# First norm and first products of a diffusion block: latent tokens ahead of context tokens, parameters loaded ahead of x

## The chip, the cores and the metric

The kernel runs on one core of a Trainium2 chip. Its engines are TensorE (PE, the matrix products; its weight loads are listed as PEld), VectorE (DVE), ScalarE (ACT), GpSimd (POOL) and SyncE (SP, which here only issues DMA transfers). The metric is the device time of one execution in microseconds; a profiled execution adds a trace in which every instruction has a start and a duration.

## The reference, cut to what matters

Two token streams share all weights: 512 latent tokens x (modulated by c) and 256 context tokens ctx (modulated by c_ctx). The change lies in the first sub-layer of layer 0, ahead of the convolutions:

```python
sh1, sc1, g1, sh2, sc2, g2 = adaln(c[:, None, :], w_mod[l], b_mod[l])   # silu(c) @ w_mod + b_mod
csh1, csc1, cg1, csh2, csc2, cg2 = adaln(c_ctx, w_mod[l], b_mod[l])
h = modulate(rmsnorm(x, norm_mix[l]), sh1, sc1)        # x * rsqrt(mean(x*x)) * gain * (1 + scale) + shift
hc = modulate(rmsnorm(xc, norm_mix[l]), csh1, csc1)
y = conv_mixers(h, w_in_ab[e], ...)                    # p = h @ w_in; v_b * sigmoid(gate_b); ...
yc = conv_mixers(hc, w_in_ab[e], ...)
```

The norm, the modulation and the products with `w_in` work on each token by itself, so latent and context tokens may be taken together or one after the other.

## The kernel before, in words

The activations lie transposed: x is eight tiles `x[k]` of 128 channels by 776 columns. Columns 0 to 511 are the latent tokens (`LAT`), 520 to 775 the context tokens (`CTXS`), and 8 columns of zeros lie between (`C0` = 520, `T` = 776).

`setup` issues all DMA transfers from SP's queue: the eight x tiles (L121), the parameters `par` (L122), the identity (L124). Behind them follow, in the order of the program, the first piece of modulation weights `wm0` (four transfers of 512 KB, L222), three tiles of `w_in` (L165), and three more pieces of `wm0`.

`start` then does the first norm and the first products. ACT squares each x[k] and DVE adds the squares up in `ss` (`square_in`, L279 to L284). `rstd` multiplies `ss` by ones on PE in chunks of 128 tokens (L291), ACT takes the means out of PSUM (L294), DVE finds the inverse root by a start value and three Newton rounds (`inverse`, L296 to L301), lays it on a diagonal `rd` (L313), and PE spreads it over all 128 partitions (L323); ACT copies the result to `r` (L432). `piece(q)` makes shift and scale of channel tiles 2q and 2q+1: 32 small products with the silu of c and c_ctx (L226), a copy (L231), a transpose (L232), a copy (L234), and on DVE `mod` (L235) and `gain` (L266).

`weights` splits each fp32 weight tile in `whi` (ACT cast, L159) and `wlo` (DVE subtract, L160), and `mod_in` does the same for the modulated activations: `xr` = x*r (L336), times gain plus shift (L345, L346, or L348), then a high part and a low part (L159, L160, or L350). Each product is three matmuls, wlo*h, whi*hl, whi*h (L177 to L179). The first three slots of PSUM take the first three column tiles of `w_in` together, tile k by tile k. Then `glu` needs the first two slots: ACT takes the sigmoid of slot two (`sg`, L561), DVE multiplies it with slot one (`ub`, L570), and this frees slot one, for which the next product waits.

Each engine works through its instructions in a fixed order, which a scheduler of the language sets at build time from the program's order and its own estimate of durations. An instruction that waits holds up all behind it on its engine.

Of the kernel before, what the change touches and what calls it, by code (L numbers as in the profile page):

```python
# [12 lines left out]
F32 = mybir.dt.float32  # L13
# [7 lines left out]
P = 128  # L21
DM = 1024
KT = DM // P
SEQ = 512
CTX = 256
GRID_W = 64
C0 = SEQ + 8
T = C0 + CTX
TW = 896
# [9 lines left out]
LAT = (0, SEQ)  # L39
CTXS = (C0, T)  # L40
# [18 lines left out]
class Kern:  # L59
# [52 lines left out]
    def setup(self):  # L112
        nc, a = self.nc, self.a
        self.cst = self.pool("cst")
        self.wts = self.pool("wts")
        self.tmp = self.pool("tmp", 2)

        self.par = self.cst.tile([P, NPAR + 64], F32, name="par")[:, :NPAR]
        self.x = [self.cst.tile([P, T], F32, name=f"x{k}") for k in range(KT)]
        for k in range(KT):  # L120
            nc.sync.dma_start(self.x[k], a["x"][:, k, :])  # L121
        nc.sync.dma_start(self.par, a["par"])  # L122
        self.ident = self.cst.tile([P, P], F32, name="ident")
        nc.sync.dma_start(self.ident, a["ident"])  # L124
        self.onesm = self.cst.tile([P, P], F32, name="onesm")
        nc.vector.memset(self.onesm, 1.0)
        self.ones2 = self.cst.tile([P, 2], F32, name="ones2")
        nc.vector.memset(self.ones2, 1.0 / DM)
        self.ones2b = self.cst.tile([P, 2], F32, name="ones2b")
        nc.vector.memset(self.ones2b, 2.0 / DM)  # L130

        self.mod = self.cst.tile([P, 2, 48, 2], F32, name="mod")

        self.gain = self.cst.tile([P, 4, KT, 2], F32, name="gain")
        self.csil = self.cst.tile([P, KT, 2], F32, name="csil")
        nc.scalar.activation(self.csil, self.p("cc").rearrange("p (k c) -> p k c", c=2), AF.Silu)
# [275 lines left out]
    def start(self, ph):  # L412

        nc, a = self.nc, self.a
        segs = [LAT, CTXS]
        self.new_ss()
        for k in range(KT):
            self.square_in(k, 0, T)
        sl = [self.slot() for _ in range(3)]
        ms = self.slot()  # L420
        nc.vector.memset(ms[:, 0:P], 0.0)

        def piece(q):
            room = lambda _: ph.tile([P, 2, 512], F32, name="wmod", tag="wmod", bufs=14)
            for _ in self.mod_piece(0, 0, 16, 2 * q, a["wm0"][q], ms[:, 0:P], ms[:, 768:768 + P], room):
                pass
            self.make_gain(0, 0, 1, self.p("nmix")[:, 0:8], 2 * q, 2 * q + 2)

        piece(0)
        rp = self.rstd(self.ss, segs, self.ones2, sl[0], eng=nc.vector, pool=ph)  # L430
        r = self.tmp.tile([P, T], F32, name="r", tag="ss", bufs=1)
        nc.scalar.copy(r, rp)  # L432
        room = [[ph.tile([P, DM], F32R, name=t) for t in ("whi0", "wlo0")], None, None]
        first = [self.weights(a["w_in"][m], into=room[m]) for m in range(3)]
        piece(1)
        h = self.new_h()
        for q in range(4):
            for k in (2 * q, 2 * q + 1):
                self.mod_in(h, k, r, 0, 0, 0, segs)
            for k in (2 * q, 2 * q + 1):  # L440
                for s, w in zip(sl, first):
                    self.wide_gemm(s, w, h, segs, [k])
            if q == 0:
                piece(2)
                piece(3)
        return h, sl
# [76 lines left out]
    def spread(self, seg, project=None):  # L523

        r = self.tmp.tile([P, SEQ], F32, name="r", tag="r", bufs=1)[:, :seg[1] - seg[0]]
        s, others = self.taken()
        self.turn(others)
        self.nc.scalar.copy(r, self.rstd(self.ss, [seg], self.ones2, s, project=project))
        i = self.slot_i % len(others)
        self.turn(others[i:] + others[:i] + [s])  # L530
        return r
# [530 lines left out]
```

## Time and profile before

| what | value |
|---|---|
| time, median of 3 runs | 1472.5 us (1471.82 to 1473.2) |
| the profiled execution, its own time | 1473.53 us |
| its span, first to last instruction | 1471.8 us |
| PE busy | 1435.4 us, 98% of the span |
| DVE busy | 1024.4 us, 70% |
| ACT busy | 596.9 us, 41% |
| DMA, mean | 110 GB/s, 33.4% of 16 engines |

The span is the time between the first and the last instruction; the execution's own time is 1.73 us longer. PE is busy nearly throughout, so time is lost mostly where PE is not yet running or waits. The trace is read at the start of the program, up to about 60 us.

### The profile page before, as it was taken

Reading aid. Unit: us, or ns where it says so; the run is one execution under the profiler, and the core shown is the slowest. Engines: PE = TensorE matmul, PEld = TensorE weight load, DVE = VectorE, ACT = ScalarE, POOL = GpSimd, SP = SyncE. Lnnn points to the kernel's source line nnn. Section 1 sums busy time; section 2 is a strip of 40 time slices with the busy share of each in tenths; the row PEclk is TensorE's granted clock in tenths of the full one; section 3 lists DMA queues with packets and bytes.
Section 4 is the critical chain, followed back from the end, with each engine's and each line's share of the span. In section 5 each row is a group of like instructions: output and inputs, shape, how many; then the busy total and the mean of one; then the engine's idle time right before and its main releaser. Section 6 shows DMA issues by size and latency. Waiting matters only on the chain.

```text
span 1471.8 us, 21937 instructions
## 1 busy us (share of the span) xinstructions
PE 1435.4 (98%) x8786; PEld 1228.8 (83%) x8786; DVE 1024.4 (70%) x1635; ACT 596.9 (41%) x983; POOL 47.8 (3%) x186
## 2 busy tenths in 40 slices
PE   5999999999999999999999999999999999999997
PEld 3888888888888888888888878768799888888887
DVE  6699998689977756456434689786676865655456
ACT  5421224463223223133123475786764442424245
POOL 0000001110000000000000110010001000000000
PEclk9999999999999999999999999999999999999999
DMA  9325433134544532333211324011155333233222
GB/s 374 111 70 173 158 115 130 31 113 146 168 132 127 186 106 81 120 125 91 81 47 43 106 91 125 14 40 58 42 174 163 90 112 98 84 114 97 94 80 74
DMA packets 52709, 161.25 MB, mean 110 GB/s; under 512 B 6400, under 2 KB 6528, under 8 KB 52480
## 3 DMA queue, kind: packets, MB, share of 16 engines
q1 hardware_dynamic: 52608, 159.87, 33.4%
q8 instruction: 68, 1.11, 0.3%
q14 instruction: 33, 0.27, 0.1%
HBM read 155.13 MB, written 2.10 MB: 107 GB/s over the span
## 4 chain that ended last, share of the span: by engine, by line
PE 91%; DVE 4%; ACT 2%; issue 1%; DMA 1%; POOL 1%; DVEq 0%; SPq 0%; ACTq 0%; POOLq 0%
PE slot L177 21%; PE slot L178 21%; PE slot L179 21%; PE av L178 3%; PE av L177 3%; PE av L179 3%; PE av L929 2%; PE pt L919 2%; PE s L900 2%; PE pt L179 2%; PE pt L178 2%; PE pt L177 2%; PE slot L226 1%; PE slot L212 1%; PE slot L208 1%
## 5 line engine op out<-in xcount | busy, mean ns | idle before, releaser
L177 PE MATMUL slot<-h,wlo 128*128 128x512 f32 (+1 forms) x1192 | 410.5, 346 | 2.2 <-DVE ub L570 1.2
L178 PE MATMUL slot<-h,whi 128*128 128x512 f32 (+1 forms) x1192 | 410.8, 345 | 0.2 <-DVE h L350 0.2
L179 PE MATMUL slot<-h,whi 128*128 128x512 f32 (+1 forms) x1192 | 410.8, 345 | 0.0
L159 ACT CAST whi<-wraw 128x1024 fp32r<-128x1024 f32 (+2 forms) x215 | 192.2, 902 | 208.5 <-PE slot L179 109.3
L177 PEld LDWEIGHTS slot<-h,wlo 128*128 128x128 f32 x1192 | 223.5, 188 | 34.3 <-issue 2.0
L178 PEld LDWEIGHTS slot<-h,whi 128*128 128x128 f32 x1192 | 224.1, 188 | 29.0 <-DVE h L350 0.5
L179 PEld LDWEIGHTS slot<-h,whi 128*128 128x128 f32 x1192 | 224.1, 188 | 27.6
L160 DVE TENSOR_TENSOR wlo<-wraw,whi 128x1024 fp32r<-128x1024 f32 (+2 forms) x215 | 222.2, 1040 | 25.1 <-ACT whi L159 24.6
L370 DVE SCALAR_TENSOR_TENSOR cf<-slot,par,cf 128x775 f32<-128x775 f32 (+1 forms) x132 | 122.7, 932 | 136.5 <-ACT cf L368 136.0
L177 PE MATMUL slot<-gh,wlo 128*128 128x512 f32 (+1 forms) x459 | 156.7, 342 | 0.7 <-DVE x L360 0.4
L178 PE MATMUL slot<-gl,whi 128*128 128x512 f32 (+1 forms) x459 | 155.5, 339 | 0.0
L179 PE MATMUL slot<-gh,whi 128*128 128x512 f32 (+1 forms) x459 | 155.1, 339 | 0.0
L368 ACT ACTIVATE cf<-slot,par 128x776 f32<-128x776 f32 (+1 forms) x66 | 55.3, 837 | 243.1 <-PE slot L179 230.7
L360 DVE SCALAR_TENSOR_TENSOR x<-slot,mod,x 128x256 f32<-128x256 f32 (+1 forms) x139 | 81.8, 618 | 73.6 <-PE slot L179 73.4
L578 DVE SCALAR_TENSOR_TENSOR cacc<-ub,par,cacc 128x783 f32<-128x783 f32 x120 | 118.6, 1040 | 0.2
L254 DVE CUSTOM_DVE_ANT_0 junk<-wmod,cb 128x1024 bf16<-128x1024 f32 x80 | 97.7, 1221 | 10.2 <-DMA wmod<-in_wmt 6.6
L177 PEld LDWEIGHTS slot<-gh,wlo 128*128 128x128 f32 x459 | 86.1, 188 | 12.0 <-DVE wlo L160 0.7
L178 PEld LDWEIGHTS slot<-gl,whi 128*128 128x128 f32 x459 | 86.4, 188 | 10.3 <-DVE mod L235 0.2
L179 PEld LDWEIGHTS slot<-gh,whi 128*128 128x128 f32 x459 | 86.4, 188 | 10.1
L907 DVE CUSTOM_DVE_ANT_0 sm<-s,mask,nsink 128x640 f32<-128x640 f32 (+1 forms) x58 | 46.8, 820 | 15.9 <-PE pt L919 12.4
L704 ACT ACTIVATE sgf<-cf 128x776 f32<-128x776 f32 (+1 forms) x44 | 32.7, 744 | 60.9 <-DVE cf L370 60.4
L910 ACT ACTIVATE sm<-sm,nm 128x513 f32<-128x513 f32 (+1 forms) x64 | 50.1, 786 | 10.6 <-DVE nm L907 5.6
(244 smaller groups left out, 2246.4 us busy)
## 6 DMA issues: line engine op xcount, KB each, us to landing
wraw<-in_w_up SPq DMA_DIRECT2D x88, 512.0 KB, 3.6
wmod<-in_wmt SPq DMA_DIRECT2D x56, 512.0 KB, 4.2
wmod<-in_wm SPq DMA_DIRECT2D x40, 512.0 KB, 5.3
wraw<-in_w_down SPq DMA_DIRECT2D x48, 256.0 KB, 2.6
wraw<-in_w_in SPq DMA_DIRECT2D x20, 512.0 KB, 4.0
wraw<-in_w_down SPq DMA_DIRECT2D x32, 320.0 KB, 2.9
wraw<-in_w_o SPq DMA_DIRECT2D x16, 512.0 KB, 3.4
wraw<-in_w_out SPq DMA_DIRECT2D x16, 256.0 KB, 3.4
```

Source lines behind the costliest of these rows:

```text
L159: self.act_mark = self.nc.scalar.copy(hi, src)
L160: self.mark = self.nc.vector.tensor_tensor(lo, src, hi.bitcast(F32), op=ALU.subtract)
L177: mm(out, lo, xh, start=first, stop=False)
L178: mm(out, hi, xl, start=False, stop=False)
L179: self.product = mm(out, hi, xh, start=False, stop=last)
L254: nc.vector.tensor_tensor_reduce(junk, w, self.cb[:, c, :], 1.0, 0.0, ALU.mult, ALU.add, col)
L360: self.nc.vector.scalar_tensor_tensor(self.x[k][:, lo:hi], acc, self.mod[:, l, chunk * 8 + k, c:c + 1], self.x[k][:, lo:hi], op0=ALU.mult, ...
L368: nc.scalar.activation(acc[:, :n], u[:, :n], AF.Copy, scale=w[:, 1:2])
L370: nc.vector.scalar_tensor_tensor(acc[:, o], u[:, i], w[:, j:j + 1], acc[:, o], op0=ALU.mult, op1=ALU.add)
L578: self.tapped = nc.vector.scalar_tensor_tensor(acc, ub[:, t:t + CB_N], w[:, t:t + 1], acc, op0=ALU.mult, op1=ALU.add)
L907: scored = nc.vector.tensor_tensor_reduce(sm[:, :n], s[:, SEQ - nl:SEQ + CTX], mk, -SCALE, nsink[:, hd:hd + 1], ALU.add, ALU.min, nm)
L910: self.scored = scored, nc.scalar.activation(sm[:, :n + 1], sm[:, :n + 1], AF.Exp, scale=-1.0, bias=nm, accum_out=z)
```

## The change: what it does

`par` is issued first. Each x tile comes in two transfers, latent columns of all eight tiles first and then columns 512 to 775 of all eight. The squares, the inverse root and the spread are done for the latent tokens; the squares of the context tokens are issued after the latent means, and their inverse root and spread come inside the loop, behind the latent products of k = 0 and 1. From then on each pair of channel tiles is modulated and multiplied for the latent tokens and then for the context tokens. Lines of the changed kernel stand 1 to 10 below those of before.

```diff
         self.x = [self.cst.tile([P, T], F32, name=f"x{k}") for k in range(KT)]
-        for k in range(KT):
-            nc.sync.dma_start(self.x[k], a["x"][:, k, :])
         nc.sync.dma_start(self.par, a["par"])
+        for lo, hi in (LAT, (SEQ, T)):
+            for k in range(KT):
+                nc.sync.dma_start(self.x[k][:, lo:hi], a["x"][:, k, lo:hi])
...
         for k in range(KT):
-            self.square_in(k, 0, T)
+            self.square_in(k, *LAT)
...
         piece(0)
-        rp = self.rstd(self.ss, segs, self.ones2, sl[0], eng=nc.vector, pool=ph)
-        r = self.tmp.tile([P, T], F32, name="r", tag="ss", bufs=1)
-        nc.scalar.copy(r, rp)
+        r = ph.tile([P, TW], F32, name="r")
+
+        def spread(seg, slot):
+            nc.scalar.copy(r[:, slice(*seg)], self.rstd(self.ss, [seg], self.ones2, slot, eng=nc.vector, pool=ph))
+
+        spread(LAT, sl[0])
+        with self.tc.issue_after(self.means.ins):
+            for k in range(KT):
+                self.square_in(k, *CTXS)
...
         for q in range(4):
-            for k in (2 * q, 2 * q + 1):
-                self.mod_in(h, k, r, 0, 0, 0, segs)
-            for k in (2 * q, 2 * q + 1):
-                for s, w in zip(sl, first):
-                    self.wide_gemm(s, w, h, segs, [k])
+            for seg in segs:
+                if q == 0 and seg == CTXS:
+                    spread(seg, sl[0][:, C0:])
+                for k in (2 * q, 2 * q + 1):
+                    self.mod_in(h, k, r[:, slice(*seg)], 0, 0, 0, [seg])
+                for k in (2 * q, 2 * q + 1):
+                    for s, w in zip(sl, first):
+                        self.wide_gemm(s, w, h, [seg], [k])
             if q == 0:
                 piece(2)
                 piece(3)
```

On DVE, between the last latent square and the inverse root, stood one run of adds and one run of Newton steps before (`ss` is the sum of squares, `ry` and `rt` the Newton variables):

```order
-L284 TENSOR_TENSOR ss<-ss,sq 128x776 x7
-L296 TENSOR_SCALAR ry<-rv 128x6
-L298 TENSOR_TENSOR rt<-ry 128x6
-L299 TENSOR_TENSOR rt<-rt,rv 128x6
-L300 TENSOR_SCALAR rt<-rt 128x6
-L301 TENSOR_TENSOR ry<-rt,ry 128x6
```

Now, at the same place on DVE:

```order
+L285 TENSOR_TENSOR ss<-ss,sq 128x512 x7
+L297 TENSOR_SCALAR ry<-rv 128x4
+L299 TENSOR_TENSOR rt<-ry 128x4
+L300 TENSOR_TENSOR rt<-rt,rv 128x4
+L285 TENSOR_TENSOR ss<-ss,sq 128x256
+L301 TENSOR_SCALAR rt<-rt 128x4
+L285 TENSOR_TENSOR ss<-ss,sq 128x256
+L302 TENSOR_TENSOR ry<-rt,ry 128x4
+L285 TENSOR_TENSOR ss<-ss,sq 128x256
```

The seven adds of the context squares (two of them shown last) stand between the Newton steps of the latent tokens.

On PE, behind the products of k = 1 (the rows named `h,whi`), the third modulation piece (L226 x32) and the products of k = 2 followed before:

```order
-L177 MATMUL slot_102<-h,wlo 128x256
-L178 MATMUL slot_102<-h,whi 128x256
-L179 MATMUL slot_102<-h,whi 128x256
-L226 MATMUL slot_103<-wmod,csil 2x128 x32
-L177 MATMUL slot_100<-h,wlo_212 128x512
-L177 MATMUL slot_101<-h,wlo 128x512
```

Now, behind the latent products of k = 1 on PE (slot_108 to slot_110 are the three slots, slot_111 the modulation's):

```order
+L179 MATMUL slot_110<-h,whi 128x512
+L180 MATMUL slot_110<-h,whi 128x512
+L292 MATMUL slot_108<-ones_94,ss 128x2 x2
+L233 MATMUL slot_111<-ident,modsb 128x128
+L227 MATMUL slot_111<-wmod,csil 2x128 x32
+L233 MATMUL slot_111<-ident,modsb 128x128
+L324 MATMUL slot_108<-rd,onesm 128x256
+L227 MATMUL slot_111<-wmod,csil 2x128 x32
+L178 MATMUL slot_108<-h,wlo_239 128x256
```

The context sums (L292) and the context spread (L324) now stand in PE's queue with two modulation pieces around them, ahead of the context products of k = 0 and with no other product between.

On ACT, behind the context spread, the queue now reads:

```order
+L434 COPY r<-slot_108 128x256
+L346 ACTIVATE h<-xr,mod,gain 128x256 x2
+L160 CAST whi<-wraw 128x1024
+L232 COPY modsb<-slot_111 128x128
+L349 ACTIVATE ht<-xr,mod,gain 128x512 x2
+L160 CAST h<-ht 128x512
```

The latent modulation of k = 2 and 3 (L349) and its first high part (L160, `h<-ht`) stand behind the context tokens' copy, the context high parts and the cast of the fourth weight tile.

## Rows read from the trace of the kernel before

**Rows 1.** The page's slices: busy tenths of PE in 40 equal parts.

```profile
PE   5999999999999999999999999999999999999997
```

**Rows 2.** Timeline, 0 to 30 us: start, duration, engine, line, count, idle before.

```profile
9.18 5.25 DVE L284 TENSOR_TENSOR ss<-ss,sq 128x776 f32<-128x776 f32 x5 [0.94 <-ACT sq L283]
...
14.49 2.72 PE L291 MATMUL slot<-ones,ss 128*128 128x2 f32 x12 [14.49 <-DVE ss L284]
...
17.14 3.47 PE L226 MATMUL slot<-wmod,csil 128*2 128x128 f32 x64
...
17.45 0.17 DVE L296 TENSOR_SCALAR ry<-rv 128x6 int32<-128x6 int32 x1 [3.02 <-ACT rv L294]
...
20.08 0.96 DVE L313 TENSOR_TENSOR rd<-ident,ry 128x768 f32<-128x768 f32 x1
...
20.96 3.49 DVE L160 TENSOR_TENSOR wlo<-wraw,whi 128x1024 fp32r<-128x1024 f32 x3
...
21.18 1.53 PE L323 MATMUL slot<-rd,onesm 128*128 128x512 f32 x4 [0.58 <-DVE rd L313]
...
22.08 1.05 ACT L159 CAST whi<-wraw 128x1024 fp32r<-128x1024 f32 x1 [0.19 <-DMA wraw<-in_w_in]
...
23.04 0.80 ACT L432 COPY r<-slot 128x776 f32<-128x776 f32 x1
...
26.51 1.66 DVE L346 TENSOR_SCALAR ht<-xr,gain,mod 128x512 f32<-128x512 f32 x4
...
28.08 0.96 DVE L350 TENSOR_TENSOR h<-ht,h 128x776 fp32r<-128x776 f32 x1
...
29.10 0.50 PE L178 MATMUL slot<-h,whi 128*128 128x512 f32 x1 [0.21 <-DVE h L350]
```

**Rows 3.** Groups by shape, 0 to 60 us: busy us, mean ns, idle before.

```profile
L570 DVE TENSOR_TENSOR ub<-slot,sg 128x512 f32<-128x512 f32 x1 | 0.7, 692 | 5.9 <-ACT sg L561 5.9
...
L570 DVE TENSOR_TENSOR ub<-slot,sg 128x256 f32<-128x256 f32 x1 | 0.4, 415 | 0.0
...
L348 ACT ACTIVATE ht<-xr,mod,gain 128x512 f32<-128x512 f32 x6 | 4.9, 811 | 1.6 <-DVE gain L266 1.6
L159 ACT CAST h<-ht 128x776 fp32r<-128x776 f32 x6 | 4.7, 836 | 0.0
L348 ACT ACTIVATE ht<-xr,mod,gain 128x264 f32<-128x264 f32 x6 | 3.6, 597 | 0.0
```

**Rows 4.** Timeline, 57 to 60 us: the end of the first products.

```profile
57.65 0.82 ACT L561 ACTIVATE sg<-slot 128x776 f32<-128x776 f32 x1 [5.06 <-PE slot L179]
57.68 0.39 PE L179 MATMUL slot<-h,whi 128*128 128x512 f32 x1
...
57.91 0.28 PE L177 MATMUL slot<-h,wlo 128*128 128x256 f32 x1
...
58.03 0.28 PE L178 MATMUL slot<-h,whi 128*128 128x256 f32 x1
...
58.15 0.28 PE L179 MATMUL slot<-h,whi 128*128 128x256 f32 x1
...
59.58 0.50 PE L177 MATMUL slot<-h,wlo 128*128 128x512 f32 x1 [1.15 <-DVE ub L570]
```

**Rows 5.** Timeline, 30 to 80 us: a whole modulation piece on PE.

```profile
35.02 1.93 PE L226 MATMUL slot<-wmod,csil 128*2 128x128 f32 x64
```

**Rows 6.** Timeline near 847 us: sums of two chunks on PE, in layer 1.

```profile
846.97 0.61 PE L291 MATMUL slot<-ones,ss 128*128 128x2 f32 x4 [1.98 <-DVE ss L284]
```

**Rows 7.** Stretches: busy of PE, PEld, DVE, ACT, POOL; clock, DMA share, GB/s.

```profile
6.00:8.00 2.00, 0.00 (x0) 0.00 (x0) 1.69 (x2) 0.85 (x1) 0.00 (x0) 1.00 1.00 366
12.00:14.00 2.00, 0.00 (x0) 0.00 (x0) 1.79 (x3) 1.76 (x3) 0.00 (x0) 1.00 1.05 417
```

**Rows 8.** The same view near 850 us: two stretches of 512-column products.

```profile
849.00:852.00 3.00, 3.00 (x10) 2.32 (x9) 2.52 (x5) 1.87 (x4) 2.83 (x3) 0.63 0.06 22
858.00:861.00 3.00, 3.00 (x15) 2.49 (x14) 2.63 (x5) 2.97 (x6) 0.00 (x0) 1.00 0.00 0
```

## The prediction

> **What bounds the kernel now.** I read the page's slices first: PE stands at 5 tenths in the first of 40 slices and at 9 nearly everywhere after it [rows 1]. So PE is the bound, and what this change can win or lose lies ahead of the point from which PE runs without gaps. The timeline of the first 30 us shows the run-up: DVE adds squares until 14.43, PE sums them until 17.2, DVE does Newton and the diagonal until 21.0, PE spreads, ACT copies r at 23.04, and the first product with a low part starts at 29.10 [rows 2]. From there PE runs through its products until 58.27 (the last 256-column product starts at 58.15 and takes its turn of 0.12), waits for the gated unit, and goes on at 59.58 [rows 4]. A delay at 59.58 is passed on to the end, because PE and DVE both start their long stretch there. My sum is the shift of this one point.
>
> **A: the start of the products.** The latent norm is shorter at each step. A DVE operation of 512 columns takes 0.69 us [rows 3] where five of 776 took 5.25, 1.05 each [rows 2]; so seven adds in a row, about 0.75 each with the wait between, end near 11.2 instead of 14.43 (x starts 0.7 later behind par, but its first tile is a third smaller). Eight sums instead of twelve at 2.72/12 = 0.23 us [rows 2] are 1.8 us on PE; the Newton steps could start at 13.3 instead of 17.45. That is 4 us won. Then it is given back. Newton took 20.08 - 17.45 = 2.6 us [rows 2]; the seven context adds stand between its steps, 0.35 us each of pipelined time, and the diagonal takes 0.69: ready at 19.0, against 21.04 before. PE holds the first modulation piece ahead of the spread; before it took 3.47 us, until 20.6 [rows 2]; its weights come behind the same bytes of x and par, so I take 19. After it the loads of `w_in` decide: ACT's third cast waited for its transfer until 22.08 [rows 2], and the second transfer of 512 KB (0.524 MB) landed 1.26 us earlier at the 417 GB/s of [rows 7], at 20.8. In the new order ACT casts tile two (to 21.9) and then copies r (512 columns, about 0.55: 22.4 against 23.84). DVE follows with wlo of tile two (23.1), two xr of 0.65, mod, wlo of tile three (25.7; three took 3.49 [rows 2]), gain, two `ht` (0.54 each instead of four in 1.66 [rows 2]) and the first low part (0.69 instead of 0.96): 27.6 or 27.7, against 29.04. **A = -1.4 us.**
>
> The unknown is how fast narrower rows of x load. Rows of 3104 bytes (776 columns) moved at 366 GB/s, rows of 4096 bytes at 417 [rows 7]. Upper bound: both new widths (2048 and 1056 bytes) move at 417; then x's 3.18 MB take 7.6 instead of 8.7 us, and everything behind is 1.1 us earlier. Lower bound: the rate falls on as it does between the two rows, by 51 GB/s per kilobyte: 312 and 261 GB/s, 6.7 + 4.1 = 10.8 us, 2.1 later. I take no shift, since 2048 bytes lie nearest to the 3104 row. A lies between -2.5 and +0.7.
>
> **B: work moved into PE's stream.** The context sums (four instructions, 0.61 [rows 6]) and the 256-column spread (a third of 1.53, so 0.5 [rows 2]) were done while PE had nothing else; now they stand between products. **B = +1.1 us.** All products keep their price: 512 columns 0.23, 256 columns 0.12 each [rows 4], also when only narrow ones follow each other. The extra instructions of DVE and ACT (an operation split in 512 and 256 columns costs about 0.15 more on DVE, 0.3 on ACT) are hidden behind 6.3 us of products per pair of tiles once PE runs; without that cover they would cost some 4 us.
>
> **C: new waits of PE.** Before, PE had wide products from 29.10 on. Now the latent products of k = 0 and 1 are 18 x 0.23 = 4.2 us, and then PE's queue holds sums, a piece, the spread, a piece, and the context products. The chain behind the sums: 0.61 sums, 0.2 means, 2.6 Newton plus 0.4 for two foreign operations between, 0.4 diagonal, with handovers 4.5 us until the spread can start. PE's own work in it: 0.61, a piece of 1.93 [rows 5], two transposes of about 0.27: 3.1. PE waits 1.4. The way on (spread, copy 0.36, xr 0.42, high part 0.6) is covered by the next piece of 1.93. Then 18 narrow products take 2.1 us, and the latent tiles of k = 2 must be ready. On ACT they stand behind two context high parts, a weight cast of 1.0, a copy, two `ht` of 0.81 [rows 3] and a cast (0.61 by width from 836 at 776 columns): about 4.5 us from the first context high part, while PE has 3.1 left. PE waits 1.4, and for the low part 0.3 more, since DVE has wlo of the fourth weight tile ahead of it. **C = +3.1 us.** Bounds: 1.4 if one of the two waits closes; 5 if the fourth weight tile, whose cast now stands ahead, lands 2 us late.
>
> **D: the end of the first products.** Before, slot two was complete 0.62 us ahead of PE's last product (sigmoid at 57.65, PE's end 58.27 [rows 4]). Now the slots end with three narrow products each, and slot two ends 3 x 0.12 ahead, less 0.2 of latency. **D = +0.5 us** of the unit's time no longer covered.
>
> **Sum:** -1.4 + 1.1 + 3.1 + 0.5 = +3.3 us. The profiled execution has a span of 1471.8 and its own time 1473.53, 1.0 above the median of the runs; I add the sum to the median 1472.5: **1475.8 us**. Later reorderings that the build makes in layer 1's query products lie where PE has no gap to fill, and cost nothing.
>
> **Rival 1, x loads at full rate: not slower by what can be told.** If narrow rows move at 417 GB/s, weights and modulation land 1.1 earlier, A is -2.5 and the sum +2.2: 1474.7. It decides when the second `w_in` tile lands before about 20.2. For it: of x, two thirds of the bytes are in rows that are half of a 4096-byte row, and the 3104-byte row is no such fraction. Against it: the one narrower row seen is slower. The Trainium skill, "DMA: Bandwidth & Descriptors", section Specifications, gives 512 bytes as the least transfer at line rate, so both widths would run at full rate; the 3104-byte rows here, at 366 against 417, do not agree with it. By that rule the sum would be +2.2 instead of +3.3.
>
> **Rival 2, the products start at half clock.** After PE had stood from 844.99 to 846.97 and again near 848, the granted clock was 0.63 over three microseconds and ten 512-column products were done where fifteen were later at 1.00 [rows 8]; the low level is 1.2 of 2.4 GHz. One such stretch costs a third of 3 us and most of that again in the next: 1.5 to 2. In the new order PE has only small modulation products between about 21 and 27, less than before, and a thin stretch again between 32 and 39. For it: that idleness. Against it: before, the products at 29.10 came after similar gaps and ran at 0.23. Sum +5: 1477.6. The Trainium skill, "TensorE: Matmul & The Clock Gate", section Why this matters for your kernels, warns of idle gaps between bursts of matmuls as what halves the clock; the trace agrees near 850.
>
> **Rival 3, narrow rows are slow:** A = +0.7, and with the fourth weight tile late too C = 4: sum +6.3, 1478.8.
>
> **Rival 4, the shorter norm carries: faster or no change.** If the 4 us won before Newton reached the products, A would be -4 and the sum -0.3 with B, C and D kept: 1472.2. It needs the second `w_in` tile, and the modulation weights ahead of it, 3 us earlier; the rows of the loads [rows 2, 7] speak against it. With C closed as well it would end near 1469.
>
> **Chances and range.** My forecast 0.42, rival 1 0.21, rival 2 0.21, rival 3 0.08, rival 4 0.08. About 0.2%, 2.9 us, is what a measurement of this kernel can tell from no change. The forecast's own spread (A -2 to -0.8, C 2 to 4: +1.6 to +4.8) puts six tenths of it above that line; with most of rivals 2 and 3 this makes slower 0.57, no change 0.35, faster 0.08. The range takes in rivals 1 to 3 and leaves out most of rival 4 and the doubled mishaps: 1473.0 to 1480.0.
>
> **What would show it.** Right: the first low-part product near 27.7; two PE waits of 1 to 2 us between 32 and 43, the first released by the diagonal, the second by ACT's cast of h; PE back from the gated unit near 63. A wrong: the second `w_in` tile lands well off 20.8. C wrong: PE goes from latent to context products without a gap, or waits over 5 us. The whole is wrong if the point at 59.58 moves by less than 2 us or the end doesn't follow it.

## The result, and the profile after

The changed kernel takes 1483.87 us (median of 6 runs, 1482.66 to 1484.14) where the kernel before takes 1472.66 (6 runs); the ratio is 1.0074 (95% interval 1.0061 to 1.0087). It is slower, as the likeliest case said, but by 11 us, not 3, and outside the range of 1473.0 to 1480.0.

The profiled execution has a span of 1480.7 us, 8.9 above that of before. Three stretches of PE's timeline make up the whole of it:

| stretch | before | after | difference | forecast |
|---|---|---|---|---|
| start of the first low-part product | 29.10 | 29.84 | +0.74 | -1.4 |
| from there to the return from the gated unit | 30.48 | 36.28 | +5.80 | +4.7 |
| from there to the end of the span | 1412.22 | 1414.58 | +2.36 | 0 |

(29.10 to 59.58 before; 29.84 to 66.12 after.) The rest up to 11.2 is spread between executions: the profiled one of after is the fastest of its six, 1.2 below their median, that of before 0.9 above its own, and 0.2 lies outside the spans.

PE's timeline of the start, with the columns of [rows 2]:

```profile
12.05 1.87 PE L292 MATMUL slot<-ones,ss 128*128 128x2 f32 x8 [12.05 <-DVE ss L285]
15.32 1.03 PE L227 MATMUL slot<-wmod,csil 128*2 128x128 f32 x16 [1.40 <-DMA wmod<-in_wm]
16.51 1.03 PE L227 MATMUL slot<-wmod,csil 128*2 128x128 f32 x16 [0.16 <-DMA wmod<-in_wm]
...
19.07 1.03 PE L227 MATMUL slot<-wmod,csil 128*2 128x128 f32 x16 [0.25 <-DMA wmod<-in_wm]
20.03 2.01 PE L324 MATMUL slot<-rd,onesm 128*128 128x512 f32 x2
...
27.30 1.65 PE L178 MATMUL slot<-h,wlo 128*128 128x512 f32 x3 [0.81 <-ACT h L346]
28.87 1.03 PE L227 MATMUL slot<-wmod,csil 128*2 128x128 f32 x16
29.84 0.79 PE L179 MATMUL slot<-h,whi 128*128 128x512 f32 x1
30.43 0.63 PE L180 MATMUL slot<-h,whi 128*128 128x512 f32 x1
30.86 0.63 PE L179 MATMUL slot<-h,whi 128*128 128x512 f32 x1
```

The latent sums start at 12.05, 2.4 us ahead of [rows 2]. But then every quarter of the first modulation piece waits for its transfer, where before the piece had no such wait, and the spread behind it ends at 22.0. The products then stand 0.43 us apart instead of 0.23, until 32.1, the three `wlo` products at 27.30 with them. On DVE the first low parts were ready earlier than PE came to them:

```profile
27.35 1.33 DVE L351 TENSOR_TENSOR h<-ht,h 128x512 fp32r<-128x512 f32 x2
```

The first of the two was done at about 28.0, near the forecast 27.6 or 27.7. But PE still had three `wlo` products and 16 modulation products ahead of it, which took 2.54 us (27.30 to 29.84); e6 below needs 1.44 for the same instructions at full rate. ACT's casts in the same stretch:

```profile
20.17 0.27 ACT L232 COPY modsb<-slot 128x128 f32<-128x128 f32 x1 [2.40 <-PE slot L227]
20.33 1.05 ACT L160 CAST whi<-wraw 128x1024 fp32r<-128x1024 f32 x1
21.60 1.04 ACT L160 CAST whi<-wraw 128x1024 fp32r<-128x1024 f32 x1 [0.23 <-DMA wraw<-in_w_in]
```

The first cast waits behind the late piece's copy, the second for its transfer: the second tile of `w_in` lands at 21.6, not at the forecast 20.8. The stretches show the load rate and the clock (columns of [rows 7]):

```profile
10.00:12.00 2.00, 0.00 (x0) 0.00 (x0) 1.79 (x3) 0.91 (x2) 0.00 (x0) 1.00 1.06 326
12.00:14.00 2.00, 1.87 (x8) 1.78 (x8) 0.00 (x1) 0.04 (x1) 0.00 (x0) 1.00 1.00 301
...
27.00:30.00 3.00, 2.70 (x20) 1.40 (x20) 1.68 (x3) 0.95 (x2) 0.00 (x0) 0.50 1.02 397
30.00:33.00 3.00, 3.00 (x9) 2.22 (x9) 0.00 (x0) 0.00 (x0) 0.00 (x0) 0.65 1.03 410
```

301 GB/s where [rows 7] had 417, and a granted clock of 0.50, the low level of 1.2 GHz, where before it was 1.00 from 24 to 36 us. The lack of bytes does not open where the latent pieces of x load: up to 10 us the same view adds up to 2.86 MB, before to 2.80. It opens from 10 to 16 us (2.02 MB, before 2.46), where the last pieces of 1056 bytes give way to the weights, whose rows are as wide as before. SP issued these weights later, because 16 transfers of x took it 9.00 us where 8 took 4.12:

```profile
1.18 9.00 SPq L123 DMA_DIRECT2D x<-in_x  x16
...
10.70 1.85 SPq L223 DMA_DIRECT2D wmod<-in_wm  x4
```

Before, the first modulation weights were issued at 6.39. No run changes the width of the rows and the number of transfers apart from each other, so which of them made the lack is not shown. PE's waits between the first latent products and the gated unit, and its return from it:

```profile
36.20 1.93 PE L227 MATMUL slot<-wmod,csil 128*2 128x128 f32 x64 [0.35 <-ACT modsb L235]
38.52 0.33 PE L233 MATMUL slot<-ident,modsb 128*128 128x128 f32 x1 [0.39 <-ACT modsb L232]
39.04 0.70 PE L324 MATMUL slot<-rd,onesm 128*128 128x256 f32 x2 [0.19 <-DVE rd L314]
42.34 0.38 PE L179 MATMUL slot<-h,whi 128*128 128x256 f32 x1 [0.18 <-DVE h L351]
45.23 0.96 PE L178 MATMUL slot<-h,wlo 128*128 128x512 f32 x3 [0.77 <-ACT h L160]
...
66.12 0.50 PE L178 MATMUL slot<-h,wlo 128*128 128x512 f32 x1 [1.61 <-DVE ub L580]
```

Both waits of step C are there, smaller than forecast (0.9 in three pieces, of which the diagonal releases the last 0.19, and 1.0 in two), and D is 1.61 - 1.15 = 0.46 against [rows 4]. The third loss is 850 us later, in layer 1's products for queries (q) and keys (K), on PE and then on ACT and DVE:

```profile
886.94 0.47 PE L178 MATMUL slot<-h,wlo 128*128 128x512 f32 x1 [1.51 <-DVE wlo L161]
893.52 0.50 PE L178 MATMUL slot<-h,wlo 128*128 128x512 f32 x1 [0.86 <-DVE kl L803]
...
880.12 0.59 ACT L768 COPY rp<-slot 128x512 f32<-128x512 f32 x1 [4.32 <-PE slot L213]
...
881.60 2.95 ACT L160 CAST whi<-wraw 128x1024 fp32r<-128x1024 f32 x3
...
885.58 1.22 DVE L161 TENSOR_TENSOR wlo<-wraw,whi 128x1024 fp32r<-128x1024 f32 x1
```

Neither wait exists before. K is finished when ACT copies it at 880.12, and PE has 23 query products (5.3 us at 0.23) left behind it; the weight of the next one, the last of three that ACT casts behind K's first copies, is ready at 886.8, 6.7 us behind the copy. Before, 36 products (8.3 us) lay behind K, and the same weight was ready 7.6 us behind K's copy. The 1.51 and 0.86 are the 2.36 of the table. That they agree so closely is in part chance: in the kernels below that keep layer 1's order, and in the kernel before, the stretch behind the return takes 1410.9 to 1413.1 us.

### The profile page after: what moved, and what is told of

It is laid out like the page before. It is cut to its first block, busy times and chain, and to the rows that moved or that the text cites. A ratio compares the mean times of both kernels' runs of the same rounds, so it can differ in the third digit from the quotient of the medians.

```text
span 1480.7 us, 22016 instructions
## 1 busy us (share of the span) xinstructions
PE 1440.1 (97%) x8786; PEld 1229.5 (83%) x8786; DVE 1028.0 (69%) x1672; ACT 597.2 (40%) x998; POOL 46.3 (3%) x186
## 4 chain that ended last, share of the span: by engine, by line
PE 89%; DVE 5%; ACT 2%; issue 2%; DMA 1%; POOL 1%; SPq 0%; DVEq 0%; ACTq 0%; POOLq 0%
PE slot L178 21%; PE slot L179 21%; PE slot L180 21%; PE av L179 3%; PE av L178 3%; PE av L180 2%; PE av L939 2%; PE pt L929 2%; PE s L910 2%; PE pt L180 2%; PE pt L178 2%; PE pt L179 2%; PE slot L213 1%; PE slot L209 1%; PE slot L210 1%
## 5 line engine op out<-in xcount | busy, mean ns | idle before, releaser
L160 ACT CAST whi<-wraw 128x1024 fp32r<-128x1024 f32 (+2 forms) x215 | 191.7, 900 | 204.3 <-PE slot L180 102.6
```

The costliest lines, as they stand in the source:

```text
L160: self.act_mark = self.nc.scalar.copy(hi, src)
```

## The experiments

Times are medians, each ratio is to the kernel before in the same job (1473.0 to 1473.7 us there); "start" is the first low-part product, "return" PE's first product behind the gated unit. e4, e5, e8, e10 and e13 change the kernel before and hold the query products as e1 does; e2, e3, e6, e9 and e12 change e1.

| kernel | us | ratio, 95% interval | start | return |
|---|---|---|---|---|
| e1_query_order | 1482.81 | 1.0065 (1.0050 to 1.0080) | 31.27 | 67.35 |
| e2_busy_pe | 1479.36 | 1.0041 (1.0026 to 1.0056) | 29.27 | 63.55 |
| e3_context_norm_first | 1479.15 | 1.0045 (1.0028 to 1.0061) | 30.07 | 65.63 |
| e4_products_only | 1473.22 | 1.0001 (0.9992 to 1.0010) | 27.72 | 59.57 |
| e5_loads_only | 1481.25 | 1.0048 (1.0035 to 1.0061) | 40.53 | 68.06 |
| e6_whole_x | 1478.21 | 1.0032 (1.0019 to 1.0044) | 27.62 | 63.17 |
| e7_queries_forward | 1473.93 | 1.0000 (0.9991 to 1.0009) | 28.92 | 59.40 |
| e8_first_pair | 1474.69 | 1.0010 (1.0001 to 1.0019) | 27.74 | 61.10 |
| e9_params_first_whole_x | 1479.01 | 1.0045 (1.0031 to 1.0058) | 28.73 | 64.30 |
| e10_narrow_x | 1475.77 | 1.0015 (1.0006 to 1.0023) | 30.63 | 61.08 |
| e11_queries_and_casts | 1476.22 | 1.0019 (1.0010 to 1.0027) | 28.68 | 59.12 |
| e12_whole_x_context_norm_first | 1478.42 | 1.0033 (1.0020 to 1.0046) | 28.31 | 64.48 |
| e13_wide_x | 1476.63 | 1.0014 (1.0005 to 1.0023) | 31.45 | 62.15 |

### The loads

**e6_whole_x**, the changed kernel with e1's query order (below) and the loads of before:

```diff
-        nc.sync.dma_start(self.par, a["par"])
-        for lo, hi in (LAT, (SEQ, T)):
-            for k in range(KT):
-                nc.sync.dma_start(self.x[k][:, lo:hi], a["x"][:, k, lo:hi])
+        for k in range(KT):
+            nc.sync.dma_start(self.x[k], a["x"][:, k, :])
+        nc.sync.dma_start(self.par, a["par"])
```

> The changed kernel with x loaded whole ahead of the parameters as before, and the query products held as in e1_query_order; norm, modulation and products still take latent, then context tokens. Against e1_query_order (+9.8 us) the loads alone differ. Theory (narrow rows cost 1 to 2 us ahead of the first products, and the late modulation is what lets PE fall to half clock): first cast back at 19.5, first low-part product near 28 to 28.5, return from the gated unit near 65 instead of 67, time +6.5 to +8.5. Rival (loads don't matter, the split norm alone does it): as e1_query_order, +9.5 to +10.

It is 4.6 us above before where e1 is 9.8 above, and its profile is nearly the one that was forecast for the change:

```profile
26.18 0.96 PE L177 MATMUL slot<-h,wlo 128*128 128x512 f32 x3 [1.24 <-ACT h L345]
27.08 0.62 PE L226 MATMUL slot<-wmod,csil 128*2 128x128 f32 x16
27.62 0.50 PE L178 MATMUL slot<-h,whi 128*128 128x512 f32 x1
...
32.94 1.93 PE L226 MATMUL slot<-wmod,csil 128*2 128x128 f32 x64 [0.35 <-ACT modsb L234]
...
63.17 0.50 PE L177 MATMUL slot<-h,wlo 128*128 128x512 f32 x1 [1.61 <-DVE ub L579]
```

Start 27.62 (forecast 27.7), return 63.17 (forecast near 63), no half clock in the products, and nothing lost behind: 1475.4 - 63.17 = 1412.2, as before. So with the loads of before, the sum of A to D holds to 0.3 us (3.6 in the span, 3.3 forecast). Against this kernel, after loses 2.95 us until the return: 1.12 up to the first `wlo` product (27.30 against 26.18), 1.10 from there to the start, for the same instructions at half rate, and 0.73 behind the start.

**e10_narrow_x**, the kernel before with each tile of x in two pieces, in place:

```diff
         for k in range(KT):
-            nc.sync.dma_start(self.x[k], a["x"][:, k, :])
+            for lo, hi in ((0, 388), (388, T)):
+                nc.sync.dma_start(self.x[k][:, lo:hi], a["x"][:, k, lo:hi])
```

> The kernel before with one thing changed: each tile of x comes as two pieces of 388 columns (1552-byte rows), one behind the other, in the same place of the queue; every engine's order as before. Theory (rows of this width load at 300 to 350 GB/s instead of 363): the 3.18 MB of x take 9 to 10.5 us instead of 8.7, the norm's sums and the first cast come 0.5 to 2 us later, and the end follows: +0.5 to +2.5 us. Rival 1 of the prediction (half-width rows at full rate, 417): +0, or a gain of up to 1 us.

+2.3 us; every engine's order is that of before, so this is the price of the split load alone: rows of half the width, and twice as many transfers. ACT's first cast and PE's two points:

```profile
21.12 1.04 ACT L160 CAST whi<-wraw 128x1024 fp32r<-128x1024 f32 x1 [3.06 <-DMA wraw<-in_w_in]
...
30.63 0.50 PE L179 MATMUL slot<-h,whi 128*128 128x512 f32 x1 [0.21 <-DVE h L351]
...
61.08 0.50 PE L178 MATMUL slot<-h,wlo 128*128 128x512 f32 x1 [1.15 <-DVE ub L571]
```

The cast waits for its transfer until 21.12 (19.52 before); start and return move by the same 1.5 (the profiled execution is one of the faster ones). Rival 1 of the prediction falls.

**e13_wide_x**, the kernel before with x in four transfers of two tiles:

```diff
-        self.x = [self.cst.tile([P, T], F32, name=f"x{k}") for k in range(KT)]
-        for k in range(KT):
-            nc.sync.dma_start(self.x[k], a["x"][:, k, :])
+        pairs = [self.cst.tile([P, 2, T], F32, name=f"x{k}") for k in range(KT // 2)]
+        self.x = [pairs[k // 2][:, k % 2, :] for k in range(KT)]
+        for k in range(0, KT, 2):
+            nc.sync.dma_start(pairs[k // 2], a["x"][:, k:k + 2, :])
```

> The kernel before with x loaded as four transfers of two tiles (rows of 6208 bytes) in the place of eight of 3104; the build moves a few modulation products of the front ahead of the norm's sums, nothing else changes. Theory (the rate of the x loads rises with the width of the row): 390 to 417 GB/s between 4 and 10 us where before had 357 to 366, everything behind x about 0.5 to 1 us earlier, first low-part product near 28.3, time 0 to -1 us. Rival (the rate between 2 and 10 us is a start-up of the queues, whatever the rows): the same 360 GB/s, first cast at 19.5, no change.

The rate behaved as the theory said, the time did not. The stretch of 6 to 8 us, and PE's front:

```profile
6.00:8.00 2.00, 0.00 (x0) 0.00 (x0) 0.97 (x1) 1.73 (x4) 0.00 (x0) 1.00 1.00 419
```

```profile
14.72 1.03 PE L227 MATMUL slot<-wmod,csil 128*2 128x128 f32 x16 [14.72 <-ACT csil L137]
15.68 2.72 PE L292 MATMUL slot<-ones,ss 128*128 128x2 f32 x12
...
26.16 2.39 PE L227 MATMUL slot<-wmod,csil 128*2 128x128 f32 x64
```

419 GB/s against 366 in [rows 7] (428 and 432 in the stretches beside it; the eight kernels with whole tiles lie between 326 and 410 from 4 to 10 us), and the first cast at 18.51. But the build, with other durations to plan by, put modulation products ahead of the sums and 64 more ahead of the first products: sums 1.2 us later than before, start at 31.45. Wider rows in fewer transfers loaded faster; this version still loses.

**e5_loads_only**, the kernel before with the change's two load edits only.

> The kernel before with the loads of the change alone: the parameters first, x in a 512-column and a 264-column piece per tile; norm, modulation and products whole as before, layer 1's query order as before (the build only puts the first modulation pieces ahead of the norm's sums). Theory (the narrow rows load slower, and this is where A was lost): the first cast of a weight tile starts 1 to 2 us later than the 19.5 of before, between 12 and 16 us the rate falls to 300 to 340 GB/s, the first low-part product moves from 29.1 to 30 to 31, and the end follows: +1 to +2 us. Rival (full-rate loads, rival 1 of the prediction): the casts stay at 19.5, no change.

+7.7 us, far more than the theory's 1 to 2. The theory left out what the edits do to a norm that stays whole. DVE's adds and PE's front:

```profile
12.05 7.41 DVE L285 TENSOR_TENSOR ss<-ss,sq 128x776 f32<-128x776 f32 x7 [10.67 <-ACT sq L284]
```

```profile
20.58 1.04 PE L227 MATMUL slot<-wmod,csil 128*2 128x128 f32 x16 [0.24 <-DMA wmod<-in_wm]
21.54 2.72 PE L292 MATMUL slot<-ones,ss 128*128 128x2 f32 x12
```

A whole square needs both pieces of its tile, and the second comes behind all eight first pieces: the adds run from 12.05 to 19.46 where before they end at 14.43. The build also put the first modulation piece, which waits for its transfers, ahead of the sums: 21.54 instead of 14.49 [rows 2]. So e5 does not price the loads; e10, whose pieces come tile by tile and whose order is that of before, does.

**e9_params_first_whole_x**, e6 with `par` ahead of x again.

> e6_whole_x (+4.7 us) with the parameters ahead of x again, x still whole: the changed kernel's order of loads, but rows of 776 columns. Theory (the width of the rows is what loads slowly; the 0.3 MB of parameters are loaded either way, only their place differs): first cast near 19.6, resume point within 1 us of e6's 63.17, +4 to +6 us. Rival (the parameters ahead of x, by delaying the norm, are what shifts the front): toward e1_query_order, +8 to +10.

It stays near e6 (return 1.1 us later; the intervals overlap), +5.6 us where e1 has +9.8. The place of `par` costs about 1 us, which is not clear of the noise; the pieces of x are the larger part.

The bytes of the first 20 us say the same of the pieces. The view of the transfers in that stretch, for e10:

```profile
DMA packets 3347, 6.31 MB, mean 316 GB/s; under 512 B 365, under 2 KB 2541, under 8 KB 3347
```

For after:

```profile
DMA packets 3408, 6.54 MB, mean 327 GB/s; under 512 B 369, under 2 KB 1521, under 8 KB 3408
```

For e13:

```profile
DMA packets 1863, 7.21 MB, mean 361 GB/s; under 512 B 197, under 2 KB 325, under 8 KB 1863
```

Before moved 6.89 MB in 2353 packets. e1, e3 and e5, with the change's pieces, moved 6.08 to 6.24. At 410 GB/s a lack of 0.35 to 0.81 MB is 0.9 to 2.0 us, the spread seen between executions with narrow rows (first cast 20.33 to 21.84 in six kernels; 19.10 to 19.99 in eight with whole tiles).

### The half clock

**e2_busy_pe**, e1 with six idle products ahead of the first ones (their result is not used):

```diff
         spread(LAT, sl[0])
+        def hot(n, rhs):
+            for _ in range(n):
+                nc.tensor.matmul(ms[:, 256:512], self.onesm, rhs, start=True, stop=True)
+        hot(3, self.x[0][:, 0:256])
+        hot(3, r[:, 0:256])
```

> As e1, and six extra 256-column fp32 products of ones into unused PSUM columns on PE between the latent spread and the first products, while PE would stand idle. They add work and no result. Theory (PE is at its low clock from about 20 to 32 us because it stands idle between 21.9 and 27.3): the first products run at 0.23 us per 512 columns, 1.5 to 2.5 us faster than e1, near 1479.5. Rival (the low clock costs nothing, since DVE's low parts set the pace there): the same as e1 or up to 1 us slower.

3.4 us less than e1 (the intervals overlap a little). The products behind:

```profile
29.27 0.50 PE L179 MATMUL slot<-h,whi 128*128 128x512 f32 x1
29.60 0.39 PE L180 MATMUL slot<-h,whi 128*128 128x512 f32 x1
29.84 0.40 PE L179 MATMUL slot<-h,whi 128*128 128x512 f32 x1
```

They run 0.23 to 0.24 apart from the second on, with a clock of 1.00 from 25 to 35. Its return is 3.80 us ahead of e1's. Of these, 0.90 stand ahead of the first `wlo` product (27.83 against 28.73): its loads were 0.9 earlier (first cast 20.86 against 21.75). From there to the start it takes 1.44 us, as e6 does, where e1 takes 2.54, as after does: 1.10 for the half clock. The other 1.80 lie behind the start (34.28 against 36.08) and are only in part the clock's: PE's waits there add up to 0.6 less than e1's, and the build interleaves the modulation in another order.

### The norm and the products

**e4_products_only**, the kernel before with loads and norm whole, modulation and products split as in the change, query order as in e1.

> The kernel before, with one part of the change alone: modulation and products of each pair of channel tiles take the latent and then the context columns; loads and norm whole, as before. Query order as in e1. Theory (the split of the products costs nothing by itself, the late context norm, the clock and the query order do): first product about 1 us earlier, end of the gated unit's wait 0.5 later, within 1 us of before, 1472 to 1473.5. Rival (the narrower instructions cost): 1476 or more.

No change. The start is 1.4 us earlier, and the split gives all of it back before the return (31.85 us in place of 30.48): a wait of 0.49 for the next pair's h, D (1.62 instead of 1.15), and 16 modulation products more behind the start.

**e8_first_pair** splits k = 0 and 1 alone:

```diff
-            for k in (2 * q, 2 * q + 1):
-                self.mod_in(h, k, r, 0, 0, 0, segs)
-            for k in (2 * q, 2 * q + 1):
-                for s, w in zip(sl, first):
-                    self.wide_gemm(s, w, h, segs, [k])
+            for part in ([LAT], [CTXS]) if q == 0 else (segs,):
+                for k in (2 * q, 2 * q + 1):
+                    self.mod_in(h, k, r[:, part[0][0]:part[-1][1]], 0, 0, 0, part)
+                for k in (2 * q, 2 * q + 1):
+                    for s, w in zip(sl, first):
+                        self.wide_gemm(s, w, h, part, [k])
```

> The kernel before with the split in latent and context tokens for the first pair of tiles alone (modulation and products of k = 0 and 1); loads, norm and the pairs behind it whole, query products held as in e1_query_order. Theory: the first low-part product starts 1.2 to 1.4 us earlier as in e4_products_only, and D (0.5 at the slots' end) is not paid: -1 to -0.5 us. Rival (the start is not what sets the resume point, since the second pair's h is late): 0 within 0.4.

The theory fell: +1.1 us. D is gone (1.15), the start is early, but PE waits for the second pair's h, which now has its full width to make while PE has only the first pair's products:

```profile
37.99 0.96 PE L177 MATMUL slot<-h,wlo 128*128 128x512 f32 x3 [1.71 <-ACT h L159]
```

**e3_context_norm_first** and **e12_whole_x_context_norm_first**, e1 and e6 with the context spread ahead of the loop:

```diff
                 self.square_in(k, *CTXS)
+        spread(CTXS, sl[0][:, C0:])
...
-                if q == 0 and seg == CTXS:
-                    spread(seg, sl[0][:, C0:])
```

> As e1, but the context tokens' inverse root and spread are issued ahead of the loop, not behind the latent products of k = 0 and 1; products still latent first. Theory (PE waits 2 to 3 us between latent and context products because the context chain starts behind them): PE has no wait between 32 and 46 us, 2 to 3.5 us faster than e1, near 1478.5. Rival (what costs is the split of the modulation and of the products in narrower instructions): the same as e1.

> e6_whole_x (+4.7 us) with the context tokens' inverse root and spread made ahead of the first products, as in e3_context_norm_first. Theory (C is what is left of the loss with x whole): the waits for the context chain go, about 1.5 to 3 us of 4.7, +1.5 to +3 us. Rival (C is only moved: the context chain delays the first latent products instead): first low-part product later by what is saved, +4 to +5.

The waits for the context chain go in both, but for 0.35. e3 gains about 3 us on e1, 3.9 in the profile, of which 1.7 lie ahead of the return and 2.2 behind it, where the edit changes nothing; e12 nothing on e6 (1.0033 against 1.0032). In e12 the start is 0.7 later, its products stand 0.43 apart until 30.2, and a new wait opens where the last pairs are made:

```profile
28.91 0.63 PE L179 MATMUL slot<-h,whi 128*128 128x512 f32 x1
29.33 0.63 PE L178 MATMUL slot<-h,whi 128*128 128x512 f32 x1
...
56.22 0.96 PE L177 MATMUL slot<-h,wlo 128*128 128x512 f32 x3 [1.06 <-ACT h L159]
```

With whole x the rival holds: C is moved, not saved. With the pieces 1.7 were gained; how much of that came from C and how much from a half rate that ended at 30.9 is not told apart.

### The queries of layer 1

**e1_query_order**, the changed kernel with most of the query products held behind the last K product (`keys`, the last product of `side_by_side`):

```diff
+        keys = self.sided
...
-            self.gemm(s[:, :SEQ], wq[i] if i < 2 else self.weights(a["w_q"][i]), h, *LAT)
+            w = wq[i] if i < 2 else self.weights(a["w_q"][i])
+            if i == 0:
+                self.gemm(s[:, :SEQ], w, h, *LAT, range(4))
+            with self.tc.issue_after(keys.ins):
+                self.gemm(s[:, :SEQ], w, h, *LAT, range(0 if i else 4, KT))
```

> The changed kernel, with the last half of the first query tile's products and all of the second's held behind the last key product of layer 1, as they stood before the change. Theory (two places: about 6.5 us at the start of the program, about 2.4 us in layer 1, where query products were drawn ahead of the key products and PE later waits 1.5 us for wlo and 0.9 us for kl): the two waits go, 2.4 us faster than the changed kernel, near 1481.5. Rival (PE waits there anyway, the gap only moves): unchanged, near 1483.9.

Both waits are gone from the trace. The time is less by some 1.4 us (11.2 and 9.8 above before), but the intervals overlap; its profiled front was 1.2 us later than that of after, and the stretch behind the return 1.5 shorter.

**e7_queries_forward**, the kernel before with the first query tile's 24 products all between the K products:

```diff
-        self.side_by_side(sl, h, segs)
+        early = self.slot()
+        self.side_by_side(sl, h, segs, lambda k: self.gemm(early[:, :SEQ], wq[0], h, *LAT, [k]))
```

> The kernel before with one thing changed, 850 us behind the front: in layer 1 the first query tile's 24 products stand between the K products, three behind the latent products of each tile, where before only 12 do (the changed kernel's build drew as many forward). Theory (the query products drawn forward are missing later as PE's filler, and their place delays K's end): front as before to 0.3 us, a new PE wait of 0.5 to 1.5 us near 885 and 893, time +1.5 to +2.4. Rival (the prediction's own sentence: PE has no gap there, order costs nothing): 0 within 0.7 us.

The rival won: no change, with a wait of 0.61 for one of ACT's copies in place of the two. But in e7 the build also moved a cast: ACT makes the first of the three query weights at 869.15, ahead of K's copies at 873.62, and the last of them is ready at 878.6, only 4.9 us behind K, while PE has 24 products (5.5 us) there. **e11_queries_and_casts** holds that one cast behind K's first copies (`after` is the copy):

```diff
-        self.split(raw[:, :n], hi[:, :n], lo[:, :n])
+        with self.tc.issue_after(after.ins) if after else nullcontext():
+            self.split(raw[:, :n], hi[:, :n], lo[:, :n])
```

> e7_queries_forward (+0.4 us) with the cast of the third query weight held behind the first copies of the finished K products on ScalarE, where the changed kernel's build has it (the kernel e7 had it ahead of them). Theory: then PE has only 24 products (5.4 us) behind K's last one, while the weight is ready some 6.8 us behind it; a PE wait of 1 to 1.5 us for wlo near 880, +1 to +2.4 us against the kernel before. Rival (the query order costs nothing wherever the casts stand): 0 within 0.7.

+2.8 us, with the two waits of after and their releasers:

```profile
879.79 0.47 PE L178 MATMUL slot<-h,wlo 128*128 128x512 f32 x1 [1.28 <-DVE wlo L160]
886.37 0.50 PE L178 MATMUL slot<-h,wlo 128*128 128x512 f32 x1 [0.89 <-DVE kl L800]
```

The three casts stand in a row again, the last weight is ready 6.7 us behind K, and PE's 24 products don't last so long. So drawing the queries forward costs 2 to 3 us where no cast is drawn forward with them. The second wait, for K's low part, was not forecast by either theory.

None of these kernels beats the kernel before.

## Why the prediction was wrong

**The step that failed is the start of the products (A), by two of its prices: "I take no shift, since 2048 bytes lie nearest to the 3104 row" and "All products keep their price: 512 columns 0.23".** A was forecast at -1.4 and measured +0.74. With whole x it is -1.48 (e6): the working of the step was right. What separates the two falls in about equal parts. 1.12 us are late operands: the second tile of `w_in` landed at 21.6 instead of 20.8, and casts, low parts and the first `wlo` product came later with it; e10 shows such a delay without anything else of the change. 1.10 us are products at 0.43 instead of 0.23 between the first `wlo` product and the start. The bound of +0.7 was reached, but not for its reason: it let x's rows load slowly, while after was level with before when the 2048-byte rows were in, and fell behind where the last pieces hand over to the weights. The sum had no term for that, nor for SP's longer row of issues.

**The half clock was a rival and came along with the slow loads.** Rivals 2 and 3 were priced as alternatives, with chances of 0.21 and 0.08. They came together here: e6, with whole x, has neither; e1 and after have both. e2 has late loads too, but its PE is kept busy, and its products run at full rate: so in e1, which differs from it by these six products alone in the source, the thin stretch ahead of the products is the cause; for after, where the same instructions take the same 2.54 us, this is argued. In after PE had thin modulation products and waits for their transfers from 15 to 27 us. Late loads alone do not bring it: e10 has them, and its first low-part products run at full rate. Nor are they needed: e12's first products were as slow with early loads. The price was forecast as 1.5 to 2, and by after and e6 it is 1.8: 1.10 ahead of the start and 0.73 behind it, where the waits of C, longer in after, have a part too.

**B, C and D held as a sum and not in their parts.** Forecast 4.7; e6 has 35.55 - 30.48 = 5.07, after 5.80 with the half clock. D was 0.46 (forecast 0.5). C's waits were 1.9 in after where 3.1 were forecast: the chain behind the context sums is shorter than taken. In e6 they were 0.9. B was larger than its 1.1: 144 modulation products stood behind the start instead of 128, besides the sums and the spread. The cost of the two edits is the one foreseen, and e4 and e12 show that it does not go away by doing one of them.

**"Later reorderings ... in layer 1's query products lie where PE has no gap to fill, and cost nothing" was wrong.** PE had no gap there because 36 products (8.3 us) lay behind K while the next weight was made in 7.6; the change left 23 (5.3 us) against 6.7. The two waits add up to 2.37 us in after, and e11 makes them from the kernel before. The sentence asked whether PE waits there before, and not for how long its ready work covers the next weight.

Added up in the profile: 1.0 for late operands and 1.1 for the half clock in A, 0.4 by which B, C and D missed and 0.7 more behind the start, 2.4 in layer 1; with the forecast of 3.3 that is the 8.9. Two other sums of the prediction do not come out, without bearing on this: rival 4 with A at -4 and 4.7 for B, C and D gives +0.7, not -0.3, and the 0.57 for slower is more than its parts (0.25 of the forecast and at most 0.29 of rivals 2 and 3). What stays open: whether the loads fell behind by the width of the row, the number of packets, or the number of transfers and the later issue of the weights, which change together in all these kernels, and why the first cast varies by 1.5 us among kernels with the same narrow loads.

## What to carry to other kernels

Splitting a load to get its first part sooner makes every row narrower and the transfers more numerous; where all loads share one busy queue, what stands behind pays, so look at when the next transfers are issued, and do not put the unknown at nothing because it lies between two bounds. Ask whether one rival feeds another: here late operands left PE thin work, and the products behind ran at half rate. A build that plans by estimated durations answers an edit at the front with new orders hundreds of microseconds on: compare all engines' orders there, and ask for each stretch how long PE's ready work lasts against when the next operand is made. A pipeline that starts earlier gains only if the second pair is ready earlier too.

## What the runs showed of the hardware

From 4 to 8 us, where x alone loads, the mean rate was 423 GB/s with rows of 6208 bytes (e13), 370 with 3104 (eight kernels, 347 to 394), 328 with 2048 (five kernels, 305 to 361) and 315 with 1552 (e10). But the narrower rows came in more transfers too, and the pieces of 1056 bytes moved at 376 GB/s from 9 to 11 us in after. The Trainium skill, "DMA: Bandwidth & Descriptors", section Specifications, gives full rate from 512 bytes on; the means here lie below the rate of the widest rows at every narrower width, without showing that the width is the cause. Its section "How a descriptor splits into AXI transactions" says that a row which does not start on a multiple of 256 bytes is fetched from the multiple below; no run here moved the starts by themselves.

SP took about half a microsecond to issue each transfer of x, whatever its size: 4 in 2.12 us (e13), 8 in 4.12 (before), 16 in 8.43 (e10) and 9.00 (after).

PE's products ran at half rate in stretches whose granted clock reads 1.00: e12's products at 28.91 and 29.33 stand 0.43 us apart, and the 16 modulation products take 1.03 us in some rows and 0.62 in others of the same kernel (e6 at 23 and 24 us). For the first products of a kernel, their spacing is the better sign than the clock's column.
